# A batched TN matmul that keeps its stores apart from its loads: four shared input slots, seven output slots, contraction in two halves

## The chip, the core and the metric

The kernel runs on one core of a Trainium2 chip. The time is the device time of one execution in microseconds (us); the median of nine executions of the kernel before is 126.8 us (126.5 to 127.23).

## The reference

```python
batch, m, k, n = 16, 512, 512, 512
a: (batch, k, m) float32      b: (batch, k, n) float32
def reference(a, b):
    return np.matmul(a.transpose(0, 2, 1), b).astype(np.float32)
```

There are sixteen products of 512x512 matrices; a comes with its contraction index first, so it can be used as the stationary operand of TensorE as it lies. The inputs are 33.55 MB, the output 16.78 MB, all float32 in HBM.

## The kernel before, in words

**Tiling.** Two matrices of the batch make a pair (G = 2), and there are eight pairs. One load brings all of a, or all of b, of one pair into an SBUF tile of 128 partitions by 16 KB (2 MB): matrix g of the pair lies in the 64 partitions from 64g on, and each partition holds R = 8 rows of the contraction index. So the 512-long contraction of one matrix is 64 partitions times 8 steps r, and a matmul has 64 rows, 128 columns of weights and 512 moving columns. The 512 output rows are split as row 4c + t, where c is the partition of the output and t = 0..3; h = t // 2 is the half of the output columns' blocks that shares a PSUM tile. A pair takes T * R * G = 64 matmuls. One store takes a whole pair, 2 MB.

**Loads and stores (SP).** There are three slots for a and three for b (NL = 3), and four for the output (NO = 4). SP's program is one list of waits and DMA issues in a fixed order (lines 65 to 85): the loads of pairs 0 to 3 first, then, for each pair i, the loads of pair i + 4, if there is one, followed by the store of pair i. `load(i)` waits until the casts of pair i - 3 are done (`s_in`, line 68); `store(i)` waits until pair i has been evicted (`s_out`, line 75). Loads and stores use the one queue of SP, so loads and stores alternate from the load of pair 4 on.

**Casts (DVE).** For each pair VectorE converts float32 into bfloat16 in four instructions of 128x2048 (lines 89 to 110): `abf0` (line 95, the weights for t = 0, 1), the two halves `bbf0` and `bbf1` of b (line 105, r = 0..3 and 4..7), and `abf1` (line 95, the weights for t = 2, 3). Each has one bfloat16 buffer, so each waits for the matmuls of the pair before (`s_mm`, lines 94 and 102). A tiny memset at line 110 reports that the pair's input slots are free.

**Matmuls (PE).** Lines 112 to 133 are a loop over the pairs. For each h it waits until the PSUM tiles of h have been evicted (`s_ev`), then runs t and r in order, with the two matrices g alternating. The whole contraction of one t is done before the next t starts. [...]

**Evictions (ACT).** ScalarE copies each PSUM tile into the output tile (line 146, 128x1024), four per pair, waits first until the store that used this output slot has landed (`s_o`, line 142), and then reports the pair (line 151). At the very start GpSimd zeroes a small block of output slot 0 and ACT stores it to HBM (lines 136 to 139, 64 KB); SP's first store waits for that (`s_w`).

Of the kernel before, what the change touches and what calls it, by code (L numbers as in the profile page):

```python
# [1 line left out]

# [4 lines left out]

@with_exitstack
def kernel(
    ctx: ExitStack,  # L10
    tc: tile.TileContext,
    a: bass.AP,
    b: bass.AP,
    out: bass.AP,
):
    nc = tc.nc
    P = 128
    batch, K, M = a.shape
    _, _, N = b.shape
    f32 = mybir.dt.float32  # L20
    bf = mybir.dt.bfloat16

    G = 2
    Q = P // G
    R = K // Q
    pairs = batch // G
    a_v = a.rearrange("(pair g) (q r) m -> pair (g q) r m", g=G, r=R)  # L30
    b_v = b.rearrange("(pair g) (q r) n -> pair (g q) r n", g=G, r=R)

    out_v = out.rearrange("(pair g) (c t) n -> pair c g t n", g=G, t=M // P)

    LAG = 4
    NL = 3
    NO = LAG
    T = M // P
    H = T // 2

    pool = ctx.enter_context(tc.tile_pool(name="sb", bufs=1))
    psum = ctx.enter_context(tc.tile_pool(name="ps", bufs=1, space=bass.MemoryType.PSUM))
    a_ts = [pool.tile([P, R, M], f32, name=f"a{j}") for j in range(NL)]
    b_ts = [pool.tile([P, R, N], f32, name=f"b{j}") for j in range(NL)]

    abf_ts = [pool.tile([P, R, M // T, 2], bf, name=f"abf{h}") for h in range(H)]
    bbf_ts = [pool.tile([P, R // 2, N], bf, name=f"bbf{v}") for v in range(2)]
    o_ts = [pool.tile([P, G, T, N], f32, name=f"o{j}") for j in range(NO)]
    dve_done = pool.tile([1, pairs], f32, name="dve_done")
    act_done = pool.tile([1, pairs], f32, name="act_done")  # L50
    ps_ts = [[psum.tile([P, 2, N], f32, name=f"ps{g}{h}") for h in range(H)] for g in range(G)]

    s_a = [tc.alloc_semaphore(f"s_a{j}") for j in range(NL)]
    s_b = [tc.alloc_semaphore(f"s_b{j}") for j in range(NL)]
    s_o = [tc.alloc_semaphore(f"s_o{j}") for j in range(NO)]
    s_in = tc.alloc_semaphore("s_in")
    s_cast = tc.alloc_semaphore("s_cast")
    s_w = tc.alloc_semaphore("s_w")
    s_z = tc.alloc_semaphore("s_z")
    s_mm = tc.alloc_semaphore("s_mm")  # L60
    s_ev = [tc.alloc_semaphore(f"s_ev{h}") for h in range(H)]
    s_out = tc.alloc_semaphore("s_out")

    with tc.tile_critical(no_gpsimd_drain=True):  # L64
        def load(i):
            j = i % NL
            if i >= NL:
                nc.sync.wait_ge(s_in, i - NL + 1)
            nc.sync.dma_start(a_ts[j][:], a_v[i]).then_inc(s_a[j], 16)
            nc.sync.dma_start(b_ts[j][:], b_v[i]).then_inc(s_b[j], 16)  # L70

        def store(i):
            if i == 0:
                nc.sync.wait_ge(s_w, 16)
            nc.sync.wait_ge(s_out, i + 1)
            nc.sync.dma_start(out_v[i], o_ts[i % NO][:]).then_inc(s_o[i % NO], 16)

        for i in range(LAG):
            load(i)
        for i in range(pairs):  # L80
            if i + LAG < pairs:
                load(i + LAG)
            store(i)
        for j in range(NO):
            nc.sync.wait_ge(s_o[j], 16 * len(range(j, pairs, NO)))

        for i in range(pairs):
            n = 16 * (i // NL + 1)
            a_f = a_ts[i % NL][:].rearrange("p r (c t) -> p r c t", t=T)
            b_f = b_ts[i % NL]  # L90

            def cast_a(h):
                if i:
                    nc.vector.wait_ge(s_mm, G * H * (i - 1) + G * (h + 1))
                nc.vector.tensor_copy(  # L95
                    out=abf_ts[h][:], in_=a_f[:, :, :, 2 * h:2 * h + 2]
                ).then_inc(s_cast, 1)

            nc.vector.wait_ge(s_a[i % NL], n)
            cast_a(0)  # L100
            if i:
                nc.vector.wait_ge(s_mm, G * H * i)
            nc.vector.wait_ge(s_b[i % NL], n)
            for v in range(2):
                nc.vector.tensor_copy(  # L105
                    out=bbf_ts[v][:], in_=b_f[:, v * (R // 2):(v + 1) * (R // 2), :]
                ).then_inc(s_cast, 1)
            cast_a(1)

            nc.vector.memset(dve_done[:, i:i + 1], 0.0).then_inc(s_in, 1)  # L110

        for h in range(H):
            nc.tensor.sem_inc(s_ev[h], 1)
        with nc.tensor.Fori(0, pairs):
            nc.tensor.wait_ge(s_cast, 1).then_inc(s_cast, -1)
            for h in range(H):
                nc.tensor.wait_ge(s_ev[h], 1).then_inc(s_ev[h], -1)
                nc.tensor.wait_ge(s_cast, 1).then_inc(s_cast, -1)  # L118
                for t in (2 * h, 2 * h + 1):
                    for r in range(R):  # L120
                        if t == 0 and r == R // 2:
                            nc.tensor.wait_ge(s_cast, 1).then_inc(s_cast, -1)
                        for g in range(G):
                            rows = slice(g * Q, (g + 1) * Q)
                            mm = nc.tensor.matmul(  # L125
                                ps_ts[g][h][:, t % 2, :],
                                abf_ts[h][rows, r, :, t % 2],
                                bbf_ts[r // (R // 2)][rows, r % (R // 2), :],
                                start=(r == 0),
                                stop=(r == R - 1),  # L130
                            )
                            if t % 2 and r == R - 1:
                                mm.then_inc(s_mm, 1)


        nc.gpsimd.memset(o_ts[0][:, 0, 0, 0:P], 0.0).then_inc(s_z, 1)  # L136
        nc.scalar.wait_ge(s_z, 1)
        nc.scalar.dma_start(out_v[0][:, 0, 0, 0:P], o_ts[0][:, 0, 0, 0:P]).then_inc(s_w, 16)
        nc.scalar.wait_ge(s_w, 16)
        for i in range(pairs):  # L140
            if i >= NO:
                nc.scalar.wait_ge(s_o[i % NO], 16 * (i // NO))
            for h in range(H):
                for g in range(G):
                    nc.scalar.wait_ge(s_mm, G * H * i + G * h + g + 1)
                    ev = nc.scalar.copy(  # L146
                        out=o_ts[i % NO][:, g, 2 * h:2 * h + 2, :], in_=ps_ts[g][h][:]
                    )
                ev.then_inc(s_ev[h], 1)

            nc.scalar.memzero(act_done[:, i:i + 1]).then_inc(s_out, 1)  # L151


# [1 line left out]
_INS = ['a', 'b']  # L155
_OUTS = [((16, 512, 512), 'float32')]


# [23 lines left out]
```

## Time and profile before

| | before |
|---|---|
| median of nine runs | 126.8 us |
| the profiled execution's own time | 127.09 us |
| its span, first to last instruction | 124.9 us |
| bytes moved / mean rate over the span | 50.40 MB / 403 GB/s |
| busy: PE, DVE, ACT | 68.6 us (55%), 37.8 us (30%), 32.8 us (26%) |
| SP queue's packets, share of 16 engines' time | 95.6% |
| mean granted TensorE clock | 0.855 |

How to read it. The profile is one execution. The span is shorter than the execution's time, since it begins with the first and ends with the last instruction. The page cuts the span into 40 equal slices and gives, for each, the busy tenths of each engine and what the 16 DMA engines moved. An engine's "idle before" names what ended its waiting. A DMA counts as landed when the last of its sixteen parts has reported; the instruction that waits for it starts then.

### The profile page before, as it was taken

How to read it: one execution, taken by the hardware profiler on the slowest of the kernel's cores; microseconds unless marked ns; L12 is line 12 of the kernel's file. 1: busy time of each engine (PE TensorE's matmuls, PEld its weight loads, DVE VectorE, ACT ScalarE, POOL GpSimd, SP SyncE). 2: the span in 40 equal slices, each digit the busy share in tenths (PEclk: the TensorE clock that was granted, in tenths of full speed). 3: DMA queues.
4: the chain of work that ended last, by engine and by line, in shares of the span. 5: the costliest groups of instructions: out<-in, count | busy, mean ns of one | idle time of the engine just before them, and what ended most of it. 6: DMA issues, size and time to landing. Idle time of an engine off the chain costs nothing. (4 is left out here: it accounts for less than half of the span.)

```text
span 124.9 us, 1277 instructions
## 1 busy us (share of the span) xinstructions
PE 68.6 (55%) x512; PEld 31.2 (25%) x512; DVE 37.8 (30%) x40; ACT 32.8 (26%) x41; POOL 0.4 (0%) x5
## 2 busy tenths in 40 slices
PE   0000199959779579659920799308990089920000
PEld 0000134325335235224500334103440034400000
DVE  0012651393383194091031900338003280000000
ACT  0000001953535514520660006600056000660000
POOL 1000000000000000000000000000000000000000
PEclk9999999999999999977999559955899855995555
DMA  4999999999999999999999999999999999999960
GB/s 89 379 429 430 451 420 435 420 430 425 435 441 435 420 420 435 380 433 430 435 441 399 449 428 430 420 404 449 428 430 404 422 435 430 422 425 425 433 281 10
DMA packets 4624, 50.40 MB, mean 403 GB/s; under 512 B 400, under 2 KB 528, under 8 KB 528
## 3 DMA queue, kind: packets, MB, share of 16 engines
q1 hardware_dynamic: 4480, 50.33, 95.6%
q10 hardware_dynamic: 144, 0.07, 0.2%
HBM read 33.55 MB, written 16.84 MB: 403 GB/s over the span
## 5 line engine op out<-in xcount | busy, mean ns | idle before, releaser
L125 PE MATMUL ps<-bbf,abf 64*128 64x512 bf16 x512 | 68.6, 430 | 41.5 <-PEq L118 41.2
L125 PEld LDWEIGHTS ps<-bbf,abf 64*128 64x128 bf16 x512 | 31.2, 105 | 78.4 <-issue 59.7
L146 ACT COPY o<-ps 128x1024 f32<-128x1024 f32 x32 | 30.8, 1016 | 58.0 <-PE ps L125 58.0
L95 DVE CAST abf<-a 128x2048 bf16<-128x2048 f32 x16 | 19.6, 1226 | 38.4 <-DMA a<-in_a_dram 28.4
L105 DVE CAST bbf<-b 128x2048 bf16<-128x2048 f32 x16 | 18.9, 1223 | 26.4 <-DMA b<-in_b_dram 22.1
L146 ACT ACT_TABLE_LOAD x1 | 1.3, 1283 | 21.4 <-PE ps L125 21.4
L151 ACT ACTIVATE act_done<-act_done 1x1 uint32<-1x1 uint32 x8 | 1.6, 198 | 0.0
L110 DVE MEMSET dve_done<- 1x1 f32 x8 | 0.5, 59 | 0.0
L136 POOL MEMSET o<- 128x128 f32 x1 | 0.2, 205 | 0.5 <-SPq L64 0.5
L166 POOL MEMSET const-bfloat16-1.0<- 128x1 bf16 x1 | 0.1, 102 | 0.0
L166 POOL MEMSET const-uint8-127<- 128x1 uint8 x1 | 0.1, 102 | 0.0
L166 POOL MEMSET const-float32-1.0<- 128x1 f32 x1 | 0.1, 100 | 0.0
L166 POOL MEMSET const-float32-0.0<- 128x1 f32 x1 | 0.1, 99 | 0.2 <-issue 0.2
## 6 DMA issues: line engine op xcount, KB each, us to landing
a<-in_a_dram SPq DMA_DIRECT2D x8, 2048.0 KB, 23.0
b<-in_b_dram SPq DMA_DIRECT2D x8, 2048.0 KB, 27.4
out_dram<-o SPq DMA_DIRECT2D x8, 2048.0 KB, 33.7
out_dram<-o ACTq DMA_DIRECT2D x1, 64.0 KB, 8.9
```

Of the source, the lines that this page charges most:

```text
L95: nc.vector.tensor_copy(out=abf_ts[h][:], in_=a_f[:, :, :, 2 * h:2 * h + 2]).then_inc(s_cast, 1)
L105: nc.vector.tensor_copy(out=bbf_ts[v][:], in_=b_f[:, v * (R // 2):(v + 1) * (R // 2), :]).then_inc(s_cast, 1)
L110: nc.vector.memset(dve_done[:, i:i + 1], 0.0).then_inc(s_in, 1)
L125: mm = nc.tensor.matmul(ps_ts[g][h][:, t % 2, :], abf_ts[h][rows, r, :, t % 2], bbf_ts[r // (R // 2)][rows, r % (R // 2), :], start=(r == ...
L136: nc.gpsimd.memset(o_ts[0][:, 0, 0, 0:P], 0.0).then_inc(s_z, 1)
L146: ev = nc.scalar.copy(out=o_ts[i % NO][:, g, 2 * h:2 * h + 2, :], in_=ps_ts[g][h][:])
L151: nc.scalar.memzero(act_done[:, i:i + 1]).then_inc(s_out, 1)
L166: nc = _bacc.Bacc("TRN2", target_bir_lowering=False, num_devices=1)
```

## The change

SP now issues all sixteen loads first and then all eight stores. The inputs share four slots of 2 MB (`x0` to `x3`): load n is a of pair n // 2 if n is even, b if odd, goes to slot n % 4, and waits from n = 4 on for the casts of load n - 4. The output has seven slots; only pair 7 uses a slot again (slot 0), and ACT waits for store 0 before it (`s_o0`). The wait `s_w` stands after all loads.

The contraction of a pair is cut into two halves v (r = 0..3 and 4..7). DVE casts half 0 of a, half 0 of b, half 1 of a, half 1 of b, each from contiguous rows, and reports a slot free after its second half, so there are two memsets per pair. The bfloat16 tiles of half 0 are free again when the matmuls of half 0 are done (new semaphore `s_v`), those of half 1 when the pair is done (`s_mm`). PE runs all four t for half 0 and then all four t for half 1, accumulating in PSUM. The weights of one t are now every fourth bfloat16 of a row; before, they were every second.

```diff
-    LAG = 4
-    NL = 3
-    NO = LAG
+    NX = 4
+    NO = pairs - 1
...
-        def load(i):
-            j = i % NL
-            if i >= NL:
-                nc.sync.wait_ge(s_in, i - NL + 1)
-            nc.sync.dma_start(a_ts[j][:], a_v[i]).then_inc(s_a[j], 16)
-            nc.sync.dma_start(b_ts[j][:], b_v[i]).then_inc(s_b[j], 16)
...
+        for n in range(2 * pairs):
+            if n >= NX:
+                nc.sync.wait_ge(s_in, n - NX + 1)
+            nc.sync.dma_start(x_ts[n % NX][:], in_v[n % 2][n // 2]).then_inc(s_x[n % NX], 16)
+        nc.sync.wait_ge(s_w, 16)
+        for i in range(pairs):
             nc.sync.wait_ge(s_out, i + 1)
-            nc.sync.dma_start(out_v[i], o_ts[i % NO][:]).then_inc(s_o[i % NO], 16)
+            nc.sync.dma_start(out_v[i], o_ts[i % NO][:]).then_inc(s_o if i else s_o0, 16)
+        nc.sync.wait_ge(s_o0, 16)
+        nc.sync.wait_ge(s_o, 16 * (pairs - 1))
...
+            for v in range(V):
+                if i and v == 0:
+                    nc.vector.wait_ge(s_v, G * i)
+                if i and v == 1:
+                    nc.vector.wait_ge(s_mm, G * H * i)
+                for n in (2 * i, 2 * i + 1):
+                    if v == 0:
+                        nc.vector.wait_ge(s_x[n % NX], 16 * (n // NX + 1))
+                    nc.vector.tensor_copy(
+                        out=(bbf_ts if n % 2 else abf_ts)[v][:],
+                        in_=x_ts[n % NX][:, v * RV:(v + 1) * RV, :],
+                    ).then_inc(s_cast, 1)
+                    if v == V - 1:
...
+                        nc.vector.memset(dve_done[:, n:n + 1], 0.0).then_inc(s_in, 1)
...
+            for v in range(V):
+                nc.tensor.wait_ge(s_cast, 2).then_inc(s_cast, -2)
+                for t in range(T):
+                    h = t // 2
+                    if v == 0 and t % 2 == 0:
+                        nc.tensor.wait_ge(s_ev[h], 1).then_inc(s_ev[h], -1)
+                    for r in range(RV):
                         for g in range(G):
                             rows = slice(g * Q, (g + 1) * Q)
+                            a_m = abf_ts[v][rows, r, :].rearrange("p (c t) -> p t c", t=T)
                             mm = nc.tensor.matmul(
                                 ps_ts[g][h][:, t % 2, :],
-                                abf_ts[h][rows, r, :, t % 2],
-                                bbf_ts[r // (R // 2)][rows, r % (R // 2), :],
-                                start=(r == 0),
-                                stop=(r == R - 1),
+                                a_m[:, t],
+                                bbf_ts[v][rows, r, :],
+                                start=(v == 0 and r == 0),
+                                stop=(v == V - 1 and r == RV - 1),
                             )
-                            if t % 2 and r == R - 1:
+                            if v == 0 and t == T - 1 and r == RV - 1:
+                                mm.then_inc(s_v, 1)
+                            if v == V - 1 and t % 2 and r == RV - 1:
                                 mm.then_inc(s_mm, 1)
...
-            if i >= NO:
-                nc.scalar.wait_ge(s_o[i % NO], 16 * (i // NO))
+            if i == NO:
+                nc.scalar.wait_ge(s_o0, 16)
```

More of the change, by code (lines that the diff above doesn't have):

```diff
@@ L28 @@
     R = K // Q
[L29 to L33, printed above, removed]
-    LAG = 4
-    NL = 3
-    NO = LAG
+    V = 2
+    RV = R // V
     T = M // P
     H = T // 2
+    pairs = batch // G
+    in_v = [x.rearrange("(pair g) (q r) m -> pair (g q) r m", g=G, r=R) for x in (a, b)]
+    out_v = out.rearrange("(pair g) (c t) n -> pair c g t n", g=G, t=T)
+    NX = 4
+    NO = pairs - 1
     pool = ctx.enter_context(tc.tile_pool(name="sb", bufs=1))
     psum = ctx.enter_context(tc.tile_pool(name="ps", bufs=1, space=bass.MemoryType.PSUM))
[L43 to L47, printed above, removed]
+    x_ts = [pool.tile([P, R, M], f32, name=f"x{j}") for j in range(NX)]
+    abf_ts = [pool.tile([P, RV, M], bf, name=f"abf{v}") for v in range(V)]
+    bbf_ts = [pool.tile([P, RV, N], bf, name=f"bbf{v}") for v in range(V)]
     o_ts = [pool.tile([P, G, T, N], f32, name=f"o{j}") for j in range(NO)]
-    dve_done = pool.tile([1, pairs], f32, name="dve_done")
+    dve_done = pool.tile([1, 2 * pairs], f32, name="dve_done")
     act_done = pool.tile([1, pairs], f32, name="act_done")
     ps_ts = [[psum.tile([P, 2, N], f32, name=f"ps{g}{h}") for h in range(H)] for g in range(G)]
-    s_a = [tc.alloc_semaphore(f"s_a{j}") for j in range(NL)]
-    s_b = [tc.alloc_semaphore(f"s_b{j}") for j in range(NL)]
-    s_o = [tc.alloc_semaphore(f"s_o{j}") for j in range(NO)]
+    s_x = [tc.alloc_semaphore(f"s_x{j}") for j in range(NX)]
+    s_o0 = tc.alloc_semaphore("s_o0")
+    s_o = tc.alloc_semaphore("s_o")
+    s_w = tc.alloc_semaphore("s_w")
+    s_z = tc.alloc_semaphore("s_z")
     s_in = tc.alloc_semaphore("s_in")
     s_cast = tc.alloc_semaphore("s_cast")
-    s_w = tc.alloc_semaphore("s_w")
-    s_z = tc.alloc_semaphore("s_z")
+    s_v = tc.alloc_semaphore("s_v")
     s_mm = tc.alloc_semaphore("s_mm")
@@ L64 @@
     with tc.tile_critical(no_gpsimd_drain=True):
-        def load(i):
-            j = i % NL
-            if i >= NL:
-                nc.sync.wait_ge(s_in, i - NL + 1)
-            nc.sync.dma_start(a_ts[j][:], a_v[i]).then_inc(s_a[j], 16)
-            nc.sync.dma_start(b_ts[j][:], b_v[i]).then_inc(s_b[j], 16)
-        def store(i):
-            if i == 0:
-                nc.sync.wait_ge(s_w, 16)
+        for n in range(2 * pairs):
+            if n >= NX:
+                nc.sync.wait_ge(s_in, n - NX + 1)
+            nc.sync.dma_start(x_ts[n % NX][:], in_v[n % 2][n // 2]).then_inc(s_x[n % NX], 16)
@@ L75, in store @@
+        nc.sync.wait_ge(s_w, 16)
+        for i in range(pairs):
             nc.sync.wait_ge(s_out, i + 1)
-            nc.sync.dma_start(out_v[i], o_ts[i % NO][:]).then_inc(s_o[i % NO], 16)
-        for i in range(LAG):
-            load(i)
+            nc.sync.dma_start(out_v[i], o_ts[i % NO][:]).then_inc(s_o if i else s_o0, 16)
+        nc.sync.wait_ge(s_o0, 16)
+        nc.sync.wait_ge(s_o, 16 * (pairs - 1))
         for i in range(pairs):
-            if i + LAG < pairs:
-                load(i + LAG)
-            store(i)
@@ L84 @@
[L84 to L110, printed above, removed]
+            for v in range(V):
[12 more added lines that the diff above has]
+                        nc.vector.memset(dve_done[:, n:n + 1], 0.0).then_inc(s_in, 1)
@@ L114 @@
         with nc.tensor.Fori(0, pairs):
[L115 to L122, printed above, removed]
+            for v in range(V):
[5 more added lines that the diff above has]
+                    for r in range(RV):
                         for g in range(G):
                             rows = slice(g * Q, (g + 1) * Q)
+                            a_m = abf_ts[v][rows, r, :].rearrange("p (c t) -> p t c", t=T)
                             mm = nc.tensor.matmul(
                                 ps_ts[g][h][:, t % 2, :],
-                                abf_ts[h][rows, r, :, t % 2],
-                                bbf_ts[r // (R // 2)][rows, r % (R // 2), :],
-                                start=(r == 0),
-                                stop=(r == R - 1),
-                            )
-                            if t % 2 and r == R - 1:
+                                a_m[:, t],
+                                bbf_ts[v][rows, r, :],
+                                start=(v == 0 and r == 0),
+                                stop=(v == V - 1 and r == RV - 1),
+                            )
+                            if v == 0 and t == T - 1 and r == RV - 1:
+                                mm.then_inc(s_v, 1)
+                            if v == V - 1 and t % 2 and r == RV - 1:
                                 mm.then_inc(s_mm, 1)
```

## The prediction, made before the result was known

> **What bounds the kernel now.** I read the page's slices first. Columns are fortieths of the 124.9 us span; the third line is the SP queue's share of the DMA engines' time.
>
> ```profile
> DMA  4999999999999999999999999999999999999960
> GB/s 89 379 429 430 451 420 435 420 430 425 435 441 435 420 420 435 380 433 430 435 441 399 449 428 430 420 404 449 428 430 404 422 435 430 422 425 425 433 281 10
> ...
> q1 hardware_dynamic: 4480, 50.33, 95.6%
> ```
>
> The DMA engines are full from the second slice to the 38th; PE is busy 55% of the span. No compute engine is the bound, and no idle slice can be filled: only the rate of moving, the first 2 us and the end are left. So I asked for the rate by stage: loads alone, loads mixed with stores (the first store is issued at 29.3), stores alone, and the end.
>
> ```profile
> 4.00:29.50 25.50, 12.91 (x94) 5.82 (x96) 9.45 (x10) 5.22 (x6) 0.00 (x0) 1.00 1.01 430
> 29.50:98.00 68.50, 46.05 (x358) 21.17 (x354) 24.89 (x26) 23.63 (x30) 0.00 (x0) 0.88 1.01 426
> 98.00:119.50 21.50, 9.65 (x64) 4.21 (x64) 3.50 (x4) 3.94 (x5) 0.00 (x0) 0.68 1.01 428
> 121.00:123.00 2.00, 0.00 (x0) 0.00 (x0) 0.00 (x0) 0.00 (x0) 0.00 (x0) 0.50 0.07 29
> ```
>
> The last column is GB/s. From 121 to 123 us 29 GB/s flow: a sixteenth of 430 is 27, so **one DMA engine is late** and the other fifteen have finished. The store's issues give the end:
>
> ```profile
> L76 SPq DMA_DIRECT2D out_dram<-o x8: 372/418/5150, 29.3 to 112.2; - x8
> ...
> DMA to landing us min/median/max: 11.3/33.7/43.1
> ```
>
> The last store is issued at 112.2, lands 11.3 later at 123.5, and 1.4 us remain to the end of the span. When did that engine fall behind? VectorE's timeline tells when loads landed, wherever a cast was waiting for one (first column: start; in brackets: idle time before it and what ended it).
>
> ```profile
> 8.80 1.23 DVE L95 CAST abf<-a 128x2048 bf16<-128x2048 f32 x1 [8.80 <-DMA a<-in_a_dram]
> ...
> 43.12 2.36 DVE L105 CAST bbf<-b 128x2048 bf16<-128x2048 f32 x2 [2.92 <-DMA b<-in_b_dram]
> ...
> 53.04 2.36 DVE L105 CAST bbf<-b 128x2048 bf16<-128x2048 f32 x2 [3.27 <-DMA b<-in_b_dram]
> ...
> 63.12 1.23 DVE L95 CAST abf<-a 128x2048 bf16<-128x2048 f32 x1 [6.57 <-DMA a<-in_a_dram]
> ...
> 78.13 1.23 DVE L95 CAST abf<-a 128x2048 bf16<-128x2048 f32 x1 [6.45 <-DMA a<-in_a_dram]
> ...
> 99.08 2.36 DVE L105 CAST bbf<-b 128x2048 bf16<-128x2048 f32 x2 [4.38 <-DMA b<-in_b_dram]
> ```
>
> Count 2 MB transfers in SP's issue order. The first is a(0), at 8.80. Line 43.12 is b(3), the 8th: 34.32 us for 7. Line 53.04 is b(4), the 10th, still with no store before it: 44.24 / 9 = 4.92 us each. From there to b(7), the 19th (three stores among them), 46.04 / 9 = **5.12 us each**. From b(7) to the last store, 24.42 / 5 = **4.88 us each**. So a transfer costs 4.9 us in a stage of one direction and 5.1 in the mixed stage: 9 times 0.2, about 2 us. The trace's sixteen landing reports of each transfer say the same: the sixteenth trails the fifteenth by 0.09 us at b(3), 0.11 at b(4), 0.26 at a(5), 0.57 at a(6), 1.06 at a(7), 1.63 at b(7), and by a constant 1.64 in stores 3 to 7.
>
> [...]
>
> **The change, part by part.** The sum is made against the profiled execution: span 124.9, its time 127.09, so 2.19 lies outside the span; the median is 0.29 below that execution, and I take 0.29 off at the end.
>
> *Order of loads and stores.* Bytes and DMAs are as before. a(0) should land at 8.80 again (same first issue; SP issues four loads at once instead of six). Fifteen more loads at 4.91 (between 34.32/7 and 44.24/9) put b(7) at 82.45. Eight stores at 4.884 put the last landing at 121.52. With 1.38 us after it the span is 122.9, that is 2.0 less. Bounds: all 23 steps at 2.097 MB / 430 GB/s = 4.877 give 120.97 (2.5 less). If the lag comes with bytes and not with mixing, nothing is gained.
>
> *Is a load ever late?* This holds only while DMA never runs dry, since no store can be issued before the last load. Let B be the landing of b of one pair; the next two loads are already queued, 9.8 us of work. DVE then casts b half 0, a half 1 and b half 1 at 1.22 each (last row; the first is for later):
>
> ```profile
> L125 PEld LDWEIGHTS ps<-bbf,abf 64*128 64x128 bf16 x512 | 31.2, 105 | 78.4 <-issue 59.7
> ...
> L105 DVE CAST bbf<-b 128x2048 bf16<-128x2048 f32 x16 | 18.9, 1223 | 26.4 <-DMA b<-in_b_dram 22.1
> ```
>
> a's slot is free at B + 2.5, b's at B + 3.7 (59 ns memsets included). An issue takes 0.4 and its data flow 1.1 later (first issue 0.94, DMA from 2.0): the data of the next load can flow at B + 4.0. The queue is empty at about B + 8.6, as landing trails the data by some 1.2 us (the first 2 MB had flowed by 7.6 by the GB/s of those stretches, and landed at 8.80). Slack: 4.6 us each pair. The slots' later release (a now waits for three casts) and the two memsets are thus free; without that cover they would cost about 1.3 us per pair.
>
> *PE.* Half 1 is cast only once the whole pair before is done (`s_mm`). PE's pairs took:
>
> ```profile
> 15.06 9.68 PE L125 MATMUL ps<-bbf,abf 64*128 64x512 bf16 x64 [15.06 <-PEq L118]
> 26.17 7.36 PE L125 MATMUL ps<-bbf,abf 64*128 64x512 bf16 x64 [1.43 <-PEq L118]
> ...
> 69.56 9.74 PE L125 MATMUL ps<-bbf,abf 64*128 64x512 bf16 x64 [6.37 <-PEq L118]
> ```
>
> A pair arrives every 9.8 us. 7.36 us is PE after short gaps, 9.7 after gaps of 6 us at a lowered clock (windows there show 0.73). Now the gap is 9.8 - 7.4 = 2.4 us, so 7.4 to 9.7, both under 9.8. Pair 0: casts at 8.80 and 13.7, PE from 14.9 to 24.6; b(1) lands at 23.5, its half 0 is cast at 24.7: on time. `s_v` (behind it: DVE's next half-0 cast of a) comes after half of PE's pair, B + 1.2 + 3.7 to 4.9, as the next a lands (B + 4.9): nothing, or up to 1.2 us inside the slack. The number of matmuls, casts and evictions is unchanged, as are the 1.22 us casts (row b shows the contiguous form).
>
> *PSUM.* h = 0 is complete at 3/4 of a pair, so its two evictions (1.016 us each) run beside the last quarter; h = 1 is evicted 2 us after the end and is needed 1.8 us into the next pair. Gap 2.4: hidden; 1 us at pair 1 with the ACT table load (1.28), also in the slack.
>
> *The tail.* Stores 0 to 6 are 34 us of DMA work. Pair 7 needs store 0 landed (about 87.3) and its matmuls (about 93); its store is due at 82.4 + 34 = 116. Hidden by over 20 us. `s_w` behind the loads: set about 10 us; nothing.
>
> Sum: 127.09 - 2.0 - 0.29 = **124.8 us**.
>
> **Rivals.**
> *Only the mean rate improves:* mixing costs all engines 426 instead of 430, 68.5 * 4 / 430 = 0.64 us, and one engine stays late for another cause: 126.2. For it: the lag grows while SP's queue is also at its deepest (an issue took 5150 ns). Against: stores alone, with that queue, add none.
> *Nothing:* lag and rate go with bytes; the order only moves them: 126.8.
> *Slower, by PE:* the load of a(7) needs the casts after pair 4, and must start to flow by 71.5 us (b(6) lands at 8.80 + 13 * 4.91 = 72.6, less the trail); less 2.8 for cast, memset and issue, PE must end pair 4 by 68.7, and (68.7 - 14.9) / 5 = **10.8 us per pair is the point**. Over it, each us per pair costs five, as all stores wait. If weights at step 4 lost their cover fully, 7.36 + 64 * 0.105 = 14.1 us per pair: pair 4 would end at 85.4, 16.7 us too late: 141.5. For it: the step is new, and PE can be starved of clock. Against: 105 ns of loading lies beside matmuls today, and 9.74 was the worst pair.
>
> **How the numbers follow.** Phases pay, 124.8 (124.2 to 125.6): 0.66. Mean rate only, 126.2: 0.12. Nothing: 0.09. Slower, 127.1 to 141.5: 0.13. A measurement tells 0.2% (0.25 us) from nothing; so faster 0.78, same 0.09, slower 0.13. Range: the low bound of the first case (124.3 by 4.877) with 0.2 to spare, up to the "nothing" case: 124.1 to 126.9.
>
> **What would show it.** Right: b(7)'s casts near 82.5; the last store landing near 121.5; no late sixteenth engine at the end (no stretch at 27 to 30 GB/s, or one under 1 us); 430 GB/s through the load stage. Wrong: a dip of GB/s before 80 us, a wait of SP for `dve_done` that outlasts the queue, PE pairs over 9.8 us, or a one-engine stretch of 2 us as before.

## The result, and the profile after

The changed kernel takes 124.81 us (median of ten runs, 124.6 to 125.19) against 126.83 us; the ratio is 0.9846, 95% interval 0.9827 to 0.9865. The forecast was 124.8. The profiled execution has a span of 122.9 us where it was 124.9.

The same lines of the page as before: busy tenths and GB/s of the DMA engines in fortieths of the span, and the share of the SP queue.

```profile
DMA  4999999999999999999999999999999999999992
GB/s 80 396 415 432 437 437 427 432 432 432 427 432 427 432 427 427 427 437 432 427 432 427 427 427 427 427 400 427 427 429 429 427 427 427 427 427 427 427 427 101
...
q1 hardware_dynamic: 4480, 50.33, 96.9%
```

As many bytes and packets flow as before (50.40 MB, 4624 packets), and DMA does not pause: from the second slice to the 39th it is never under 396 GB/s. The difference is in the last three columns: 433, 281, 10 before, 427, 427, 101 now, and the slices are shorter. The stages, with GB/s in the last column (loads alone up to about 82, stores alone after it, then the end):

```profile
4.00:30.00 26.00, 12.95 (x100) 6.83 (x102) 9.67 (x13) 5.10 (x6) 0.00 (x0) 1.00 1.01 430
30.00:60.00 30.00, 22.91 (x210) 14.43 (x208) 15.24 (x19) 11.56 (x16) 0.00 (x0) 1.00 1.01 428
60.00:80.00 20.00, 14.62 (x122) 8.24 (x120) 8.95 (x12) 7.51 (x10) 0.00 (x0) 0.91 1.00 427
...
84.00:118.00 34.00, 6.97 (x64) 4.28 (x61) 1.85 (x4) 4.61 (x7) 0.00 (x0) 0.65 1.01 428
...
120.00:121.00 1.00, 0.00 (x0) 0.00 (x0) 0.00 (x0) 0.00 (x0) 0.00 (x0) 0.50 0.49 205
121.00:122.00 1.00, 0.00 (x0) 0.00 (x0) 0.00 (x0) 0.00 (x0) 0.00 (x0) 0.50 0.00 0
```

After 121 us nothing flows, where before one engine went on for 2 us (29 GB/s from 121 to 123). VectorE's timeline gives the landings (start, duration, and in brackets the idle time before the cast and what ended it):

```profile
8.92 1.23 DVE L85 CAST abf<-x 128x2048 bf16<-128x2048 f32 x1 [8.92 <-DMA x<-in_a_dram]
...
43.19 1.23 DVE L85 CAST bbf<-x 128x2048 bf16<-128x2048 f32 x1 [3.35 <-DMA x<-in_b_dram]
...
52.98 1.23 DVE L85 CAST bbf<-x 128x2048 bf16<-128x2048 f32 x1 [3.36 <-DMA x<-in_b_dram]
...
58.19 1.23 DVE L85 CAST abf<-x 128x2048 bf16<-128x2048 f32 x1 [1.70 <-PE ps L106]
...
82.34 1.23 DVE L85 CAST bbf<-x 128x2048 bf16<-128x2048 f32 x1 [1.83 <-DMA x<-in_b_dram]
```

b(7) lands at 82.34, its sixteenth report standing at 82.32. From a(0) that is 73.42 us for 15 loads, 4.89 each, with no 5.1 anywhere. Line 58.19 shows the changed order on DVE: a(5) has landed by then, and its cast waits for the matmuls of half 0 of the pair before (the new `s_v`), 1.70 us, of which the flow shows nothing (428 GB/s from 30 to 60 us).

The trace's sixteen landing reports of each transfer, worked out as the time from the first to the sixteenth and from the fifteenth to the sixteenth:

```
spread of the 16 reports / last gap, us      kernel before         changed kernel
loads a(0) to b(3), about                    0.61 / 0.10           0.87 / 0.25
a(5)                                         0.88 / 0.26           0.86 / 0.26
a(6)                                         1.29 / 0.57           0.86 / 0.24
b(7)                                         2.63 / 1.63           0.86 / 0.26
last store                                   2.75 / 1.64           0.91 / 0.14
```

The last landing moves from 123.48 to 121.43, by 2.05 us: the first report of the last store comes 0.21 us earlier (120.73 and 120.52), and the spread behind it is 1.84 us smaller. This is the whole gain of 2.0 us of span.

The trace also has every packet of a transfer (loads 16 KB, stores 8 KB), and at the end of each engine's part one of 4 bytes. By these the late engine of the kernel before falls behind in loads alone: its gap to the fifteenth is 0.44 us at the end of b(5), 0.87 at b(6), 1.63 at b(7), and each store in between ends with the gap that it began with.

### The profile page after: what moved, and what is told of

Its sections match the earlier page's. It is cut to its first block, busy times and chain, and to the rows that moved or that the text cites. A ratio compares the mean times of both kernels' runs of the same rounds, so it can differ in the third digit from the quotient of the medians.

```text
span 122.9 us, 1258 instructions
## 1 busy us (share of the span) xinstructions
PE 60.3 (49%) x512; PEld 35.3 (29%) x512; DVE 37.9 (31%) x48; ACT 31.8 (26%) x41; POOL 0.4 (0%) x5
## 2 busy tenths in 40 slices
DMA packets 4624, 50.40 MB, mean 410 GB/s; under 512 B 400, under 2 KB 528, under 8 KB 528
## 3 DMA queue, kind: packets, MB, share of 16 engines
q1 hardware_dynamic: 4480, 50.33, 96.9%
## 5 line engine op out<-in xcount | busy, mean ns | idle before, releaser
L106 PE MATMUL ps<-bbf,abf 64*128 64x512 bf16 x512 | 60.3, 392 | 30.7 <-PEq L101 29.0
L106 PEld LDWEIGHTS ps<-bbf,abf 64*128 64x128 bf16 x512 | 35.3, 112 | 55.2 <-issue 38.1
L129 ACT COPY o<-ps 128x1024 f32<-128x1024 f32 x32 | 30.1, 1027 | 38.7 <-PE ps L106 38.7
L85 DVE CAST abf<-x 128x2048 bf16<-128x2048 f32 x16 | 19.6, 1224 | 25.2 <-PE ps L106 16.3
L85 DVE CAST bbf<-x 128x2048 bf16<-128x2048 f32 x16 | 19.6, 1225 | 22.8 <-DMA x<-in_b_dram 22.8
```

The lines of the kernel that those rows point to most:

```text
L85: nc.vector.tensor_copy(out=(bbf_ts if n % 2 else abf_ts)[v][:], in_=x_ts[n % NX][:, v * RV:(v + 1) * RV, :],).then_inc(s_cast, 1)
L106: mm = nc.tensor.matmul(ps_ts[g][h][:, t % 2, :], a_m[:, t], bbf_ts[v][rows, r, :], start=(v == 0 and r == 0), stop=(v == V - 1 and r == R ...
L129: ev = nc.scalar.copy(out=o_ts[i % NO][:, g, 2 * h:2 * h + 2, :], in_=ps_ts[g][h][:])
```

## The experiments

Each run is compared with runs of the kernel before on the same chip. "Border" means a place in SP's order where a load stands behind a store.

**1. The changed kernel with stores among the loads again (e1).** Everything else stays.

```diff
-        for n in range(2 * pairs):
+        def load(n):
...
-        for i in range(pairs):
+        def store(i):
...
+        for i in range(pairs + 3):
+            if i < pairs:
+                load(2 * i)
+                load(2 * i + 1)
+            if i >= 3:
+                store(i - 3)
```

> The changed kernel with only SP's order put back: the store of pair i stands behind the loads of pair i + 3, so that stores and loads alternate; slots, casts and matmuls stay those of the change. Theory (order): one DMA engine falls behind while its loads run beside other engines' stores, so the time goes back to that of the kernel before, 126.3 to 127.2 us, with a stretch of over 1 us at 27 to 35 GB/s at the end. Rival (shape): the gain comes from the shared slots, the shallower load queue or the halved contraction; then this stays at 124.6 to 125.2 us and the end has no such stretch.

Measured: 126.76 us, ratio to before 1.0007 (0.9989 to 1.0024). The gain is gone, which speaks for the order and against the slots and the halves. But the windows show a second cause in this run, a dip ahead of the last store:

```profile
115.00:116.00 1.00, 0.00 (x0) 0.00 (x0) 0.00 (x0) 0.71 (x2) 0.00 (x0) 1.00 0.76 320
116.00:117.00 1.00, 0.00 (x0) 0.00 (x0) 0.00 (x0) 0.00 (x0) 0.00 (x0) 1.00 0.60 254
```

Pair 7 was evicted only at 115.7, so the last store came late: (430 - 320 + 430 - 254) / 430 = 0.7 us. The spread of the reports was 2.2 us in the three stores ahead of the last. The expected stretch of over 1 us with one engine at the end did not show (270 GB/s from 121 to 122 us, 25 in the next). So run 3 repeats the test without the dip.

**2. The kernel before with only the order changed (e2).** Two slots each for a and b make room for seven output slots; old casts, old matmuls.

```diff
-    NL = 3
-    NO = LAG
+    NL = 2
+    NO = pairs - 1
...
-        for i in range(LAG):
-            load(i)
-        for i in range(pairs):
-            if i + LAG < pairs:
-                load(i + LAG)
-            store(i)
+        for i in range(pairs):
+            load(i)
+        for i in range(pairs):
+            store(i)
```

> The kernel before with only the order changed: all loads, then all stores; to make room for seven output slots it has two slots each for a and b instead of three; its casts and matmuls stay, with the whole contraction of one t at a time. Theory (order): 124.6 to 125.3 us, since slots are free 3.7 us after b lands and the queue then still holds about 5 us of work. Rival (shape): 126.4 to 127.2 us, since nothing but the order was taken over. Third possibility: without the halves the slots come free too late, SP's loads leave gaps, and the time is over 127.5 us.

Measured: 124.65 us, ratio 0.9838 (0.9813 to 0.9862), as the changed kernel. Every transfer's reports lie within 0.54 us. So the order and the buffers that it needs are enough; the halved contraction and the shared slots add nothing that can be measured here.

**3. The order of the kernel before exactly, in the changed kernel (e7).** As run 1 with a lag of 4 pairs.

```diff
-        for i in range(pairs + 3):
+        for i in range(pairs + 4):
...
-            if i >= 3:
-                store(i - 3)
+            if i >= 4:
+                store(i - 4)
```

> The changed kernel with SP's order of the kernel before exactly: the store of pair i behind the loads of pair i + 4, so three stores have loads behind them (three borders from stores to loads) and the last store is ready in time. It is the run with a lag of 3 pairs (e1) without that run's thin queue before the last store. Theory (order): 126.0 to 127.0 us, all of it lag, no dip of GB/s before 120 us. Rival: what e1 lost was mostly its late last store; then 125.0 to 125.6 us here.

Measured: 126.68 us, ratio 0.9983 (0.9964 to 1.0002). The end of this run, in the windows' form:

```profile
112.00:118.00 6.00, 0.00 (x0) 0.00 (x0) 0.00 (x0) 0.00 (x0) 0.00 (x0) 0.67 1.01 427
...
120.00:121.00 1.00, 0.00 (x0) 0.00 (x0) 0.00 (x0) 0.00 (x0) 0.00 (x0) 0.50 0.62 262
121.00:122.00 1.00, 0.00 (x0) 0.00 (x0) 0.00 (x0) 0.00 (x0) 0.00 (x0) 0.50 0.12 49
122.00:123.00 1.00, 0.00 (x0) 0.00 (x0) 0.00 (x0) 0.00 (x0) 0.00 (x0) 0.50 0.06 25
```

There is no dip ahead of the last store; two engines (49 GB/s, a sixteenth of 427 being 27), then one (25 GB/s), run on alone. The spread of the reports is 0.5 us up to the first store, 2.43 us at b(7), and 2.5 in all later stores. With run 2 this completes the comparison: old and new compute with the mixed order 126.83 and 126.68, with the separate order 124.65 and 124.81.

**4. One block of four stores inside the loads (e3).** 12 loads, 4 stores, 4 loads, 4 stores.

> The changed kernel with one block of stores inside the loads: 12 loads, 4 stores, 4 loads, 4 stores. Theory (order, by borders): an engine falls behind only in loads that run while the other engines store, and the lag grows with every border from stores to loads; one such border costs little: the sixteenth landing report trails by under 0.6 us, 124.9 to 125.6 us. Rival (order, by bytes): every load that comes after a first store costs 0.2 us more, as in the sum of the prediction; four loads and four stores then cost 1.0 to 1.6 us, 125.8 to 126.4 us.

Measured: 125.35 us, ratio 0.9895 (0.9868 to 0.9921), inside the first range; but the last gap of the reports went to 0.72, not below 0.6. The spread goes from 0.66 to 1.16 in the first load behind the block and stays there (1.25 in b(7), 1.36 in the last store). The four loads do not each pay 0.2 us: nearly all of the price falls on the border.

**5. More borders with the same bytes (e8).** As run 3 with each store cut into two of 1 MB, one behind each load: seven borders.

```diff
-            nc.sync.dma_start(out_v[i], o_ts[i % NO][:]).then_inc(...)
+            nc.sync.dma_start(out_v[i][:, g], o_ts[i % NO][:, g]).then_inc(...)
...
+            for g in range(G):
+                if i < pairs:
+                    load(2 * i + g)
+                if i >= 4:
+                    store(i - 4, g)
```

> As the run with a lag of 4 pairs, but each store is issued as two of 1 MB, one behind each load: the same bytes are mixed, with seven borders from stores to loads instead of three. Theory (borders): each border leaves a further 0.5 to 0.65 us of lag, so 2 us or more over the run with a lag of 4: 128 to 129.5 us. Rival (bytes or time in the mixed stage): the same as the run with a lag of 4, within 0.3 us, 126.0 to 127.0 us.

Measured: 126.63 us, ratio 0.9989 (0.9971 to 1.0007). My reading by borders missed: seven cost no more than three. The reports say where it stops. Behind the first three borders the spread of the loads is 1.25, 1.91 and 2.48 us, 0.6 more each time from 0.67; behind the next four it is 2.46, 2.76, 2.83 and 2.89. So in this run a border cost about 0.6 us until the engines were some 2.5 us apart, and then hardly more. That is no fixed price: behind the three borders of run 3 the spread at the b loads is 0.59, 1.03 and 2.43 us, in the kernel before 0.98, 1.54 and 2.63.

**6. Loads and stores mixed packet by packet (e5).** ACT issues each store on its own queue.

```diff
+            nc.scalar.wait_ge(s_out, i + 1)
+            nc.scalar.dma_start(out_v[i], o_ts[i % NO][:]).then_inc(s_o if i else s_o0, 16)
```

> The changed kernel with the stores issued by ACT on its own DMA queue as soon as a pair is evicted, so that loads and stores are mixed packet by packet and not transfer by transfer. Loads then take longer and end late, with pair 7's matmuls, evictions and store uncovered behind them: 127 to 133 us in all. Theory (engines fall out of step at transfers of alternating direction): here all engines mix alike, and the sixteen landing reports of the loads stay within 1.2 us. Rival (mixing as such makes one engine slow): the loads' reports spread over 2 us or more.

Measured: 131.7 us, ratio 1.0385 (1.0324 to 1.0446). The loss is the uncovered end, as expected; the GB/s of the slices, whose last six show DMA waiting for pair 7:

```profile
GB/s 91 399 419 440 434 419 440 434 419 386 424 439 419 432 432 442 419 432 427 447 414 427 432 447 407 445 417 452 422 419 429 437 414 434 424 275 0 81 404 162
```

The loads' reports stay within 0.73 us through the whole mixed stage. So in this run reading and writing at once did not by itself make an engine late. What is left is that it takes engines which are at different transfers of different direction; this is an inference of mine from the spread of 2.43 us in run 3 and of 0.73 here, and no run isolates it.

**7. Three input slots instead of four (e4).**

```diff
-    NX = 4
+    NX = 3
```

> The changed kernel with three input slots instead of four. By the slack that the prediction worked out, a third slot less takes 4.9 us of queued work away: a's slot is free 2.4 us after b lands, its next load flows 1.1 us later at B + 3.5, and the queue is empty at B + 3.7. So it is just covered: 124.7 to 125.5 us. Rival (the fourth slot carries the gain): DMA runs dry once in each pair for 0.5 us or more, 127 us and over, with dips in GB/s in the load stage.

Measured: 140.47 us (135.67 to 143.63), ratio 1.0973 (1.0918 to 1.1028). I was wrong by 15 us. The page (of an execution of 135.67 us, the fastest of the six):

```profile
GB/s 98 395 453 407 456 294 431 436 314 426 412 309 304 461 402 358 436 426 333 417 421 176 319 421 441 319 299 360 431 424 426 431 429 429 429 431 424 426 419 51
```

The load stage has a dip for every pair. The first one close up (GB/s last; b(1) was issued at 15.98, as SP's timeline shows):

```profile
17.00:18.00 1.00, 1.00 (x6) 0.36 (x4) 0.08 (x2) 0.00 (x0) 0.00 (x0) 1.00 1.46 426
18.00:19.00 1.00, 1.00 (x8) 0.48 (x6) 0.00 (x0) 0.00 (x0) 0.00 (x0) 1.00 0.62 164
19.00:20.00 1.00, 1.00 (x14) 0.56 (x10) 0.00 (x0) 0.00 (x0) 0.00 (x0) 1.00 0.69 279
20.00:21.00 1.00, 1.00 (x12) 0.58 (x10) 0.39 (x1) 0.00 (x0) 0.00 (x0) 1.00 1.17 492
```

Full flow comes back only at about 20, 4 us after the issue, and b(1) lands at 24.52. By the trace's packets the sixteen engines finish the load before between 17.66 and 18.04 and begin b(1) between 17.8 and 18.7, 1.8 to 2.7 us after the issue, not 1.1; and twelve of the sixteen first packets take 1.0 to 1.8 us, where the median load packet of the changed kernel takes 0.61. The spread of the reports reaches 3.7 us in this run: the engines start unevenly.

**8 and 9. Four slots, released later (e10, e11).** VectorE repeats a cast two or three times into a spare tile before it reports both slots free (extra work, not part of the result).

```diff
+                        for d in range(2):          # 3 in e11
+                            if i or d:
+                                nc.vector.wait_ge(s_sp, 2 * i + d)
+                            nc.vector.tensor_copy(
+                                out=spare[:], in_=x_ts[n % NX][:, RV:, :]
+                            ).then_inc(s_sp, 1)
```

> The changed kernel with its input slots released later: VectorE repeats the cast of b's second half twice into a spare tile before it reports both slots free (extra work, the result is unchanged). Loads are then issued about 6.2 us after b lands instead of 2.4 and 3.6, some 2.4 us before the queue is empty. Theory A (1.1 us from issue to data, as the prediction took it): covered, 124.6 to 125.2 us. Theory B (the run with three slots shows 2.5 us or more, and unequal among the engines): the edge, 124.8 to 128 us.

> As the run before with three repeated casts: loads are issued about 7.4 us after b lands, some 1.2 us before the queue is empty, as in the run with three slots. Theory A (1.1 us from issue to data): just covered, 124.7 to 125.5 us. Theory B (2.5 us or more): DMA runs dry in every pair, 129 to 142 us, with dips of GB/s after each issue. Theory C (the three slots were slow for a cause of their own, not for the short queue): 124.7 to 125.5 us here.

Measured: e10 125.3 us, ratio 0.9921 (0.9889 to 0.9952); e11 130.92 us, ratio 1.0291 (1.0219 to 1.0363). e11 decides for theory B, against A and C. Its loads are issued 7.2 and 7.6 us after b lands, the first of them only 1.0 to 2.0 us before the first engine runs out of data (21.03 against 22.68 in the first pair, by the packets), and most pairs lose over a microsecond:

```profile
23.61 1.23 DVE L87 CAST bbf<-x 128x2048 bf16<-128x2048 f32 x1 [1.49 <-DMA x<-in_b_dram]
...
34.71 1.23 DVE L87 CAST bbf<-x 128x2048 bf16<-128x2048 f32 x1 [2.79 <-DMA x<-in_b_dram]
...
45.18 1.23 DVE L87 CAST bbf<-x 128x2048 bf16<-128x2048 f32 x1 [2.17 <-DMA x<-in_b_dram]
...
54.96 1.23 DVE L87 CAST bbf<-x 128x2048 bf16<-128x2048 f32 x1 [1.48 <-DMA x<-in_b_dram]
```

11.10, 10.47 and 9.78 us between landings of b, and 11.00, 11.55 and 11.13 in the rest of the timeline. In the first pair the engines begin the new load 1.9 to 2.9 us after its issue.

e10 settles less than its median suggests, which lies 0.1 us over the range of theory A and inside that of B. Its loads are issued 6.0 to 6.8 us after b lands, 2.4 us or more before the first engine runs out (29.80 against 32.17 is the closest), and no pair loses anything there. One step is lost all the same: b(6) lands 10.66 us behind b(5) where all others take 9.79. But b(6) was issued at 59.09, over 7 us before its turn at 66.4. The last packet of one engine took 1.27 us in it, and it begins just as a DMA packet of the kind "instruction" ends in the trace (71.17 to 71.48); only e10 and e11, whose program for VectorE is longer, have such a packet inside the kernel. Whether that is the cause is not shown. So issues 2.4 us or more ahead were in time, and of the six at 1.0 to 2.0 us ahead (e11) all but one were followed by a longer step (10.47 to 11.55 us where e10 has 9.79).

**10. Without the small first store (e6), and the same in the kernel of run 2 (e9).**

```diff
-        nc.gpsimd.memset(o_ts[0][:, 0, 0, 0:P], 0.0).then_inc(s_z, 1)
-        nc.scalar.wait_ge(s_z, 1)
-        nc.scalar.dma_start(out_v[0][:, 0, 0, 0:P], o_ts[0][:, 0, 0, 0:P]).then_inc(s_w, 16)
-        nc.scalar.wait_ge(s_w, 16)
...
-        nc.sync.wait_ge(s_w, 16)
```

> The changed kernel without the small first store: no zeroing of a block of slot 0 by GpSimd, no 64 KB store by ACT, no wait for it. Theory (DMA-bound from end to end): 0.07 MB less at 430 GB/s is 0.15 us less, 124.5 to 124.8 us. Rival: the first store costs nothing, [...]; then 124.8 us or more, up to 125.5.

> The kernel before with all loads first and two slots each for a and b (the run e2), and without the small first store. If both hold, it is the fastest: 124.3 to 124.6 us, against 124.65 for e2 and 124.81 for the changed kernel; if the first store costs nothing, 124.65 as e2.

Measured: e6 124.56 us, ratio 0.9819 (0.9794 to 0.9844); e9 124.44 us, ratio 0.981 (0.9785 to 0.9835). Both medians lie in the expected ranges, 0.25 us under the changed kernel and 0.21 under e2, where 64 KB at 430 GB/s would take 0.15; but the intervals overlap with those of e2 and of the changed kernel, so the gain of leaving the store out is likely and not shown. e9 has the lowest median of all: the old compute, all loads first, no first store.

## Why the prediction was right, point by point

- **The path.** DMA alone sets the time in both kernels: it is full from end to end (the SP queue's packets take 95.6% and 96.9% of the engines' time), and old and new compute give the same time in the same order (runs 2 and 3). Right.
- **Loads at 4.91, stores at 4.884.** b(7) was put at 82.45 and landed at 82.34; the last landing was put at 121.52, and by the trace's reports it is 121.43. Right, and run 2 and run 3 show that the order is the cause. That the sum hit to 0.01 us is luck: 1.9 us lie outside the span now and not 2.19, and that the profiled execution is now no longer above the median makes up for it.
- **Where the 2.0 us lay.** The count by landings was right, since a landing is the slowest engine's: b(7) of the kernel before has its first report at 96.36 and its sixteenth at 98.99, and its cast starts at 99.08. The mean rate was a small part of it: I had set 430 GB/s against 426, but the changed kernel's loads flow at 428 and 427 from 30 us on. The rival "mean rate only" was worth about 0.2 us (the first report of the last store), not 0.64.
- **That a mixed transfer costs 0.2 us more** was an average, not a law. One border cost about 0.5 us (run 4); several led to a spread of 2.2 to 2.9 us (runs 1, 3, 5), by unequal steps, and seven cost no more than three.
- **PE.** The gap was put at 2.4 us and the pair at 7.4 to 9.7. Measured, by PE's timeline (eight pairs, 7.10 to 8.96 us, gaps of 1.18 to 2.69):

```profile
34.93 7.10 PE L106 MATMUL ps<-bbf,abf 64*128 64x512 bf16 x64 [1.71 <-PEq L101]
44.71 7.10 PE L106 MATMUL ps<-bbf,abf 64*128 64x512 bf16 x64 [2.69 <-PEq L101]
...
74.08 8.60 PE L106 MATMUL ps<-bbf,abf 64*128 64x512 bf16 x64 [2.69 <-PEq L101]
```

The longest pair is the first, at a granted clock of 1.00. The first pair before, 9.68 us, had 1.00 too: that 9.7 us comes with a lowered clock was read rightly for the later pairs alone (8.77 to 9.74 us at 0.73 to 0.83).
- **Weights at step 4.** The group of weight loads now reads

```profile
L106 PEld LDWEIGHTS ps<-bbf,abf 64*128 64x128 bf16 x512 | 35.3, 112 | 55.2 <-issue 38.1
```

112 ns against 105 over the whole span, which mixes clocks. In pairs at a granted clock of 1.00 it is 110 (44 to 52 us) against 94 (25 to 34 us before): a load took 16 ns longer with the weights 8 bytes apart than with 4, though no run changes the step alone. The matmuls of a pair are no slower for it (7.10 against 7.36 us). The rival "slower, by PE" had no part: the longer loads stayed beside matmuls. That they would was my estimate; no trace of the kernel before shows the new step.
- **The slack of the loads: the term that was mis-sized.** I took 0.4 us for the issue and "data flow 1.1 later" from the first bytes of the kernel, and came to 4.6 us of slack. By runs 8 and 9 I estimate that here a load must be issued between 2.0 and 2.4 us before the first engine runs out, not 1.5: 2.4 us or more lost nothing, and at 1.0 to 2.0 us five of six steps were longer. The changed kernel issues the first load of a pair 6.0 us before (26.03 against 32.01, by the packets), so the slack is 3.6 to 4.0 us. It was still enough, and run 2, with 4.7 us or more, lost nothing either. But one slot fewer takes 4.9 us away, more than there is, and costs 15.7 us. Engines that had run dry began 1.9 to 2.9 us after the issue (e11, first pair).
- **What stays open.** Why engines that are a little apart drift further when loads and stores alternate, and why they stop at 2.2 to 2.9 us. The packets tell where the time goes. In the kernel before every store packet takes 0.31 to 0.34 us, but near the changes of direction single load packets take up to 1.13 us instead of 0.61; with all loads first the longest behind the start is 0.67 (changed kernel) and 0.62 (run 2). Most of what the late engine loses in b(5), b(6) and b(7) is one packet in each, of 0.82, 0.91 and 1.13 us, near the end of its load, while on average about 6, 12 and 14 of the other engines were already storing. Why such a packet is slow is not shown: from 36 us on in run 6, load packets beside four to nine storing engines took 0.61 us like all others.

## What to carry to other kernels

When DMA is full from end to end, look at the last engine and not only at the mean: a tail at a sixteenth of the rate (29 of 430 GB/s), and landings that come slower than bytes divided by rate (5.12 us where 2.097 MB at 430 GB/s is 4.88), were the signs here that the engines were out of step. If the output fits in SBUF beside the inputs, try all loads first and then all stores on one queue: here that kept the sixteen reports within 1 us (0.93 at most in the changed kernel, 0.54 in run 2). What it needed was only enough buffers that the compute never held back a load. Issue each load about 3 us before the queued work runs out (an estimate with some to spare: 2.4 us was enough in e10, 1.0 to 2.0 too little in five of six steps of e11), and measure the distance to that edge by delaying the release.

## What the runs showed of the hardware that I had not expected

- In e4 loads that were issued a little too late cost more than the delay alone: by my estimate 0.7 us was missing in the first pair (17.66 less 15.98 is 1.7 us ahead, and 2.4 was in time in e10), and the cost was 1.5 us a pair (b(7) lands at 93.13 and not at 82.34, over seven pairs). There twelve of sixteen first packets took 1.0 to 1.8 us instead of 0.61, and the engines restarted unevenly (spread up to 3.7 us).
- Loads alone and stores alone ran at the same rate, 427 to 430 GB/s; it was mainly the spread of the engines that differed between the orders (2.75 against 0.91 us in the last store).
- Seven changes from store to load cost no more than three (e8 and e7): 126.63 against 126.68 us.
- Stores never widened the late engine's gap in the kernel before; only loads near a change of direction did (0.44, 0.87, 1.63 us behind the b loads, unchanged through the stores).
